# One decay matrix for both directions of the chunk outputs, D times x on VectorE, five buffers for chunk operands

## The chip, the cores and the metric

The kernel runs on one NeuronCore of a Trainium2 chip. The metric is device time in microseconds (us) of one execution. Engines are called as the profile calls them: PE (TensorE), DVE (VectorE), ACT (ScalarE), POOL (GpSimd), SP (the queue that issues nearly all DMAs).

## The reference, cut to what matters

The reference is one layer of a bidirectional diffusion trunk over 256 context and 1024 latent tokens: a combined input projection, three token mixers side by side (SSD, gated MLP, S5), an output projection and an MLP. The change lies in the SSD mixer alone, which runs a chunked scan once forward and once backward over chunks of 128 tokens. For one direction, chunk and head:

```python
seg = a_cum[:, :, :, None] - a_cum[:, :, None, :]
lmat = jnp.exp(jnp.where(lower, seg, -jnp.inf))
cb = jnp.einsum('bcqgn,bckgn->bcqkg', cm, bm)
y_diag = jnp.einsum('bcqkg,bcqkgr,bckgrp->bcqgrp', cb, lmat, x * dt)
chunk_states = jnp.einsum('bckgn,bckgr,bckgrp->bcgrpn', bm, decay_to_end, x * dt)
h_next = chunk_decay * h + chunk_states
y_off = jnp.einsum('bcqgn,bcgrpn,bcqgr->bcqgrp', cm, h_prev, jnp.exp(a_cum))
y = y_diag + y_off
```

The two directions have their own dt and decay, and the mixer's sum is y_forward + flip(y_backward) + D * x. There are 8 heads of 64 channels in two groups of 4 heads; B and C are shared by the heads of a group.

## The kernel before, in words

All matrices are kept with channels on the partitions. `xbc_slab` writes x, B and C of the whole sequence to the scratch tensor `xbc_d` in DRAM, `dt_chain` makes per-token decays: `DTD` (dt), `col` (cumulated decay as a column), `wdec` (decay to the end of the chunk; for the backward direction already times dt), `dtot` (decay of a whole chunk) and, in DRAM, `rows_d` (cumulated decay as rows).

`ssd_group(pool, g)` returns two generators for a group g. `right` walks over the chunks from the right and keeps the backward state at each boundary (`hb`). `outputs` walks over the 10 chunks from the left (`NCH`), makes y of a chunk in both directions and updates the forward state `hf`. For one chunk, `outputs` does this (lines 864 to 912):

- loads `xc` (x, B, C of the chunk: 4 x 128x128, 256 KB) and `rb` (rows of decay for two directions and 4 heads, spread over 128 partitions, 512 KB); `xc` and `rb` have three buffers each
- ACT makes `er`, the exponentials for the states' part (line 876); ACT and DVE form the smaller of the two directions' exponents, 4 instructions each (879, 880), ACT takes its exponential (881). The result in `rb[:, 1]` holds the forward decays above the diagonal and the backward ones below it
- PE transposes x and B (`tok_major`, `ps_wa`), and multiplies B by C (883)
- `cm` is that product under the two triangular masks (885); DVE and POOL each multiply the decays by one half of it (887), so that there is one matrix per direction and head; DVE makes `xd`, x times dt for both directions (889)
- PE sums in `py`: D times x through a diagonal matrix `diagd` (893), and for each direction and head one matmul with `xd` as weights (896); then the states' part in `po` (903)
- DVE scales `po` (905), adds `py` (906), POOL adds the second direction (908), and the result is stored to `y_d` (909)
- `new_state` updates the forward state, for which POOL weights `xd` by `wdec` (831)

The main program (lines 1043 to 1089) runs `outputs` of group 0 among the z products, the S5 products and the states of group 1, then `outputs` of group 1 among what is left of z and the first output products. `step(n)` puts n pieces of the adaLN product (a load of 256 KB of `ada_w` and four small matmuls, line 170) behind each chunk. A Python scheduler orders the instructions on each engine when the program is built (`schedule_with_timeline_sim`); on the chip each engine and the SP queue runs its own list in order, held by semaphores. An fp32 matmul leaves two records in the trace, a transpose one.

Of the kernel before, what the change touches and what calls it, by code (L numbers as in the profile page):

```python
# [10 lines left out]
F32 = mybir.dt.float32  # L11
# [31 lines left out]
def trunk_kernel(ctx: ExitStack, tc: tile.TileContext, I, O):  # L43
# [9 lines left out]
    def tt(out, a, b, op, eng=V):  # L53
        eng.tensor_tensor(out=out, in0=a, in1=b, op=op)  # L54
# [658 lines left out]
    def dt_chain():  # L713
# [36 lines left out]
        tt(wdec[:, 1], wdec[:, 1], DTD[:, 1], ALU.mult)  # L750
# [57 lines left out]
    def ssd_group(pool, g):  # L808
# [3 lines left out]
        def chunk_xbc(c, n):  # L812
            o = xoff(c)
            xc = pool.tile([128, 4, 128], F32, tag="xc", name="xc", bufs=3)[:, 0:n]
            load(xc, xbc_d[g, 0:n, :, o:o + 128].rearrange("a p n -> p a n"))
            return xc
# [12 lines left out]
        def new_state(tag, bufs, d, c, px, bt, h, name):  # L829
            xw = pool.tile([128, 4, 64], F32, tag="xw", name="xw", bufs=2)  # L830
            tt(xw, px, scal(wdec, d, c).unsqueeze(2).to_broadcast([128, 4, 64]), ALU.mult, V if d else G)
# [30 lines left out]
        def outputs():  # L862
            hf = None
            for c in range(NCH):
# [21 lines left out]
                for d, E in ((0, V), (1, G)):  # L886
                    tt(rb[:, d], rb[:, 1], cm[:, d].unsqueeze(1).to_broadcast([128, 4, 128]), ALU.mult, E)
                xd = pool.tile([128, 2, 4, 64], F32, tag="xd", name="xd", bufs=2)
                tt(xd, px.unsqueeze(1).to_broadcast([128, 2, 4, 64]),
                   DTD[:, :, c * 8 + g * 4:c * 8 + g * 4 + 4].unsqueeze(3).to_broadcast([128, 2, 4, 64]), ALU.mult)  # L890
                py = bank("wb", 2)[:, 0:256].rearrange("p (a q) -> p a q", a=2)
                for a in range(2):
                    T.matmul(py[:, a, :], lhsT=diagd[:, 2 * g + a, :], rhs=xc[:, a], start=True, stop=False)
                    for d in range(2):
                        for par in range(2):
                            T.matmul(py[par * 64:(par + 1) * 64, a, :], lhsT=xd[:, d, 2 * a + par],
                                     rhs=rb[:, d, 2 * a + par], start=False, stop=(d == 1))
# [8 lines left out]
                tt(cm, er[:, dirs[0]], py, ALU.add)  # L906
                if len(dirs) == 2:
                    tt(cm, cm, er[:, 1], ALU.add, G)
                load(y_d[g * 256:(g + 1) * 256].rearrange("(a p) n -> p a n", p=128)[:, :, c * 128:(c + 1) * 128], cm)
                if c < NCH - 1:  # L910
                    hf = new_state("hf", 2, 0, c, xd[:, 0], bt, hf, "hf")
# [131 lines left out]
    with tc.tile_pool(name="pd", bufs=1) as pd, banks("psB"):  # L1043
        diagd = pd.tile([128, 4, 128], F32, name="diagd")
        for i in range(4):
            G.tensor_scalar(out=diagd[:, i], in0=ident, scalar1=dcol[:, i:i + 1], scalar2=None, op0=ALU.mult)
# [546 lines left out]
```

## Time and profile before

| | us |
|---|---|
| median of 3 runs | 1590.81 (1589.42 to 1593.71) |
| the profiled execution | 1586.03 |
| its span in the trace | 1584.2 |
| PE busy in the span | 1459.8 (92%) |
| DVE busy | 1075.9 (68%) |
| ACT busy | 723.0 (46%) |
| POOL busy | 447.5 (28%) |
| mean busy share of the DMA engines' main queue | 46.9% |

The busy times are over the whole span, of which the changed part of the program takes some 210 us. A busy PE is not PE at its peak: its records overlap, and each stretch has a granted clock, 1.00 for 2.4 GHz and 0.50 for 1.2 GHz; a mean between them is a mixture. In a row of a group the count is followed by busy time, mean ns of one, and the idle time of the engine just before the group with what ended it. "L896" is line 896 of the kernel before; lines of small helpers (L54, L57, L60, L48) collect many operations, which the names tell apart.

### The profile page before, as it was taken

To read this page: it belongs to the slowest core of one execution; us is meant where nothing else is said; L and a number is where in the kernel's file an instruction comes from. 1 tells how busy PE (TensorE), PEld (TensorE's weight loads), DVE (VectorE), ACT (ScalarE), POOL (GpSimd) and SP (SyncE) were. 2 spreads that over 40 slices of the span, in tenths; PEclk is the share of its full clock that TensorE was granted. 3 is DMA by queue.
4 is the path that set the end of the run, shared out by engine and by line. 5 is a ranking of instruction groups with operands and counts; after the bars stand their busy time and mean duration, and the time that the engine had idled before them with its cause. 6 is when DMAs were issued, how large, how long until landed. Compare 5 with 4: busy or idle time off the path is not lost.

```text
span 1584.2 us, 24203 instructions
## 1 busy us (share of the span) xinstructions
PE 1459.8 (92%) x8664; PEld 1226.9 (77%) x8664; DVE 1075.9 (68%) x1807; ACT 723.0 (46%) x1428; POOL 447.5 (28%) x537
## 2 busy tenths in 40 slices
PE   4789988999897889989999999999899999999895
PEld 4677877877674668878888888888788988887795
DVE  5885587575755665558977765674554768979945
ACT  3565534463533533436655554455646333424322
POOL 4875376624333331321100000000240313032023
PEclk9699999999997889999999999999999999999897
DMA  9414546368778677446444443444844245415302
GB/s 325 141 68 135 179 149 192 86 182 216 208 261 210 204 246 235 121 123 192 130 156 150 149 141 116 137 140 141 264 132 161 67 160 171 123 54 180 113 34 100
DMA packets 238808, 249.12 MB, mean 157 GB/s; under 512 B 15808, under 2 KB 165344, under 8 KB 238688
## 3 DMA queue, kind: packets, MB, share of 16 engines
q1 hardware_dynamic: 222592, 230.32, 46.9%
q10 hardware_dynamic: 16096, 17.27, 3.2%
q8 instruction: 68, 1.11, 0.3%
q14 instruction: 52, 0.43, 0.1%
HBM read 178.63 MB, written 68.89 MB: 156 GB/s over the span
## 4 chain that ended last, share of the span: by engine, by line
PE 59%; DVE 8%; DMA 6%; issue 2%; ACT 2%; POOL 1%; SPq 0%; DVEq 0%; ACTq 0%; POOLq 0%
PE ps_w L1193 7%; PE ps_w L1194 7%; PE ps_w L1192 7%; PE ps_w L1349 6%; PE ps_w L1348 6%; PE ps_w L1350 6%; PE ps_mm L221 4%; PE ps_mm L219 4%; PE ps_mm L220 4%; DMA xc<-xbc_d 2%; DVE X L54 2%; PE ps_mm L1350 1%; PE ps_mm L1349 1%; PE ps_mm L1348 1%; DMA rb<-rows_d 1%
## 5 line engine op out<-in xcount | busy, mean ns | idle before, releaser
L219 PE MATMUL ps_mm<-hi,wh 128*128 128x512 f32 (+1 forms) x576 | 211.8, 368 | 6.4 <-DVE dtr L686 2.8
L221 PE MATMUL ps_mm<-hi,wl 128*128 128x512 f32 (+1 forms) x576 | 209.4, 364 | 0.9 <-DVE wl L54 0.9
L220 PE MATMUL ps_mm<-lo,wh 128*128 128x512 f32 (+1 forms) x576 | 209.8, 364 | 0.2 <-DVE lo L54 0.2
L1348 PE MATMUL ps_w<-uB,uA 128*128 128x512 f32 (+1 forms) x520 | 190.7, 371 | 9.3 <-ACT uB L60 8.9
L1349 PE MATMUL ps_w<-uB,uA 128*128 128x512 f32 (+1 forms) x520 | 191.7, 369 | 7.7 <-DVE uB L54 7.7
L1350 PE MATMUL ps_w<-uB,uA 128*128 128x512 f32 (+1 forms) x520 | 190.5, 367 | 0.0
L54 POOL TENSOR_TENSOR cb<-h 128x512 f32<-128x512 f32 x14 | 21.1, 1512 | 512.5 <-DMA h<-w 402.7
L219 PEld LDWEIGHTS ps_mm<-hi,wh 128*128 128x128 f32 x576 | 111.2, 193 | 24.7 <-DVE dtr L686 3.2
L221 PEld LDWEIGHTS ps_mm<-hi,wl 128*128 128x128 f32 x576 | 110.9, 193 | 19.1 <-issue 2.4
L220 PEld LDWEIGHTS ps_mm<-lo,wh 128*128 128x128 f32 x576 | 111.1, 193 | 15.9 <-issue 1.2
L1348 PEld LDWEIGHTS ps_w<-uB,uA 128*128 128x128 f32 x520 | 99.9, 193 | 25.4 <-ACT uB L60 9.3
L1349 PEld LDWEIGHTS ps_w<-uB,uA 128*128 128x128 f32 x520 | 100.1, 192 | 24.5 <-DVE uB L54 9.6
L1350 PEld LDWEIGHTS ps_w<-uB,uA 128*128 128x128 f32 x520 | 100.0, 192 | 15.4
L54 DVE TENSOR_TENSOR uB<-tb,uB 128x512 fp32r<-128x512 f32 x106 | 88.7, 857 | 13.5 <-ACT uB L60 13.5
L60 ACT ACTIVATE uB<-tb 128x512 fp32r<-128x512 f32 x106 | 65.6, 625 | 62.1 <-PE ps_w L1350 31.7
L54 DVE TENSOR_TENSOR wl<-wraw,wh 128x1024 fp32r<-128x1024 f32 x32 | 50.3, 1572 | 40.6 <-ACT wh L60 40.2
L54 DVE TENSOR_TENSOR X<-X,ps_w 128x512 f32<-128x512 f32 x84 | 56.1, 680 | 27.7 <-PE ps_w L1350 27.6
L54 DVE TENSOR_TENSOR q<-q,ps_w 128x512 f32<-128x512 f32 x48 | 32.9, 686 | 60.2 <-PE ps_w L1194 59.5
L60 ACT ACTIVATE c<-c 128x512 f32<-128x512 f32 x64 | 40.3, 629 | 56.9 <-DVE c L54 55.9
L54 POOL TENSOR_TENSOR sq<-sq 128x512 f32<-128x512 f32 (+1 forms) x31 | 41.1, 1331 | 81.8 <-ACT sq L60 81.3
L1350 PE MATMUL ps_mm<-ch,uA 128*128 128x256 f32 x224 | 63.2, 283 | 0.0
L1349 PE MATMUL ps_mm<-cl,uA 128*128 128x256 f32 x224 | 63.2, 283 | 0.0
(430 smaller groups left out, 3993.9 us busy)
## 6 DMA issues: line engine op xcount, KB each, us to landing
rw<-w SPq DMA_DIRECT2D x112, 256.0 KB
tb<-a_d SPq DMA_DIRECT2D x106, 256.0 KB
aw<-ada_w SPq DMA_DIRECT2D x64, 256.0 KB
h<-w SPq DMA_DIRECT2D x32, 512.0 KB
a_d<-t SPq DMA_DIRECT2D x42, 256.0 KB
rb<-rows_d SPq DMA_DIRECT2D x20, 512.0 KB
adaw<-ada_w SPq DMA_DIRECT2D x32, 256.0 KB
wraw<-w_out SPq DMA_DIRECT2D x16, 512.0 KB
```

Of the source, the lines that this page charges most:

```text
L54: eng.tensor_tensor(out=out, in0=a, in1=b, op=op)
L60: S.activation(out=out, in_=in_, func=func, **kw)
L219: T.matmul(out, lhsT=wh(k), rhs=xh(k), start=(k == 0), stop=False)
L220: T.matmul(out, lhsT=wh(k), rhs=xl(k), start=False, stop=False)
L221: T.matmul(out, lhsT=wl(k), rhs=xh(k), start=False, stop=(k == nk - 1))
L1192: T.matmul(out, lhsT=wh, rhs=X[0][:, j, :], start=(j == 0), stop=False)
L1193: T.matmul(out, lhsT=wh, rhs=X[1][:, j, :], start=False, stop=False)
L1194: T.matmul(out, lhsT=wl, rhs=X[0][:, j, :], start=False, stop=(j == 3))
L1348: T.matmul(out, lhsT=wh, rhs=bh, start=start, stop=False)
L1349: T.matmul(out, lhsT=wh, rhs=bl, start=False, stop=False)
L1350: T.matmul(out, lhsT=wl, rhs=bh, start=False, stop=stop)
```

## The change

It makes one matrix per head out of both directions' halves, with dt in it: ACT scales the forward half of `cm` by the forward dt of each token, DVE adds the backward half times its dt, 4 instructions of 128x128 each, and one DVE product with the decays follows. x goes to PE as it is, through a copy by ACT (`xs`). D times x leaves PE: DVE adds it to `py` with two instructions per chunk. POOL now adds the two directions of the states' part before DVE adds them to the rest. The weighting `xw` of the forward state moves from POOL to DVE and reads x from PSUM, and `wdec` carries dt for both directions. `diagd` goes. `xc` has five buffers.

```diff
--- before.py
+++ after.py
@@ -747,7 +747,7 @@
         S.copy(col[:, 0], pc[:, 0:80])
         act(col[:, 1], pc[:, 80:160], ACT.Copy, scale=-1.0)
         act(wdec.rearrange("p d c -> p (d c)"), pc[:, 160:320], ACT.Exp)
-        tt(wdec[:, 1], wdec[:, 1], DTD[:, 1], ALU.mult)
+        tt(wdec, wdec, DTD, ALU.mult)
         act(dtot.rearrange("p d c -> p (d c)"), pc[:, 320:480], ACT.Exp)
         pr = bank("ad")
         for d in range(2):
@@ -811,7 +811,7 @@
 
         def chunk_xbc(c, n):
             o = xoff(c)
-            xc = pool.tile([128, 4, 128], F32, tag="xc", name="xc", bufs=3)[:, 0:n]
+            xc = pool.tile([128, 4, 128], F32, tag="xc", name="xc", bufs=5)[:, 0:n]
             load(xc, xbc_d[g, 0:n, :, o:o + 128].rearrange("a p n -> p a n"))
             return xc
 
@@ -828,7 +828,7 @@
 
         def new_state(tag, bufs, d, c, px, bt, h, name):
             xw = pool.tile([128, 4, 64], F32, tag="xw", name="xw", bufs=2)
-            tt(xw, px, scal(wdec, d, c).unsqueeze(2).to_broadcast([128, 4, 64]), ALU.mult, V if d else G)
+            tt(xw, px, scal(wdec, d, c).unsqueeze(2).to_broadcast([128, 4, 64]), ALU.mult)
             pst = bank("ws")[:, 0:256]
             T.matmul(pst, lhsT=bt, rhs=xw.rearrange("p h e -> p (h e)"), start=True, stop=True)
             hn = pool.tile([128, 256], F32, tag=tag, name=name, bufs=bufs)
@@ -883,18 +883,19 @@
                 T.matmul(pcb, lhsT=xc[:, 2], rhs=xc[:, 3], start=True, stop=True)
                 cm = pool.tile([128, 2, 128], F32, tag="cm", name="cm", bufs=2)
                 tt(cm, pcb.unsqueeze(1).to_broadcast([128, 2, 128]), tri[:, 0:2], ALU.mult)
-                for d, E in ((0, V), (1, G)):
-                    tt(rb[:, d], rb[:, 1], cm[:, d].unsqueeze(1).to_broadcast([128, 4, 128]), ALU.mult, E)
-                xd = pool.tile([128, 2, 4, 64], F32, tag="xd", name="xd", bufs=2)
-                tt(xd, px.unsqueeze(1).to_broadcast([128, 2, 4, 64]),
-                   DTD[:, :, c * 8 + g * 4:c * 8 + g * 4 + 4].unsqueeze(3).to_broadcast([128, 2, 4, 64]), ALU.mult)
+
+                d0, d1 = scal(DTD, 0, c), scal(DTD, 1, c)
+                for hh in range(4):
+                    act(rb[:, 0, hh], cm[:, 0], ACT.Copy, scale=d0[:, hh:hh + 1])
+                    stt(rb[:, 0, hh], cm[:, 1], d1[:, hh:hh + 1], rb[:, 0, hh], ALU.mult, ALU.add)
+                tt(rb[:, 1], rb[:, 1], rb[:, 0], ALU.mult)
+                xs = pool.tile([128, 4, 64], F32, tag="xs", name="xs", bufs=2)
+                S.copy(xs, px)
                 py = bank("wb", 2)[:, 0:256].rearrange("p (a q) -> p a q", a=2)
                 for a in range(2):
-                    T.matmul(py[:, a, :], lhsT=diagd[:, 2 * g + a, :], rhs=xc[:, a], start=True, stop=False)
-                    for d in range(2):
-                        for par in range(2):
-                            T.matmul(py[par * 64:(par + 1) * 64, a, :], lhsT=xd[:, d, 2 * a + par],
-                                     rhs=rb[:, d, 2 * a + par], start=False, stop=(d == 1))
+                    for par in range(2):
+                        T.matmul(py[par * 64:(par + 1) * 64, a, :], lhsT=xs[:, 2 * a + par], rhs=rb[:, 1, 2 * a + par],
+                                 start=True, stop=True)
                 hs_ = (hf, hb[c])
                 dirs = [d for d in range(2) if hs_[d] is not None]
                 po = bank("wb", 2).rearrange("p (d a q) -> p d a q", d=2, a=2)
@@ -903,12 +904,14 @@
                         T.matmul(po[:, d, a], lhsT=hs_[d][:, a * 128:(a + 1) * 128], rhs=xc[:, 3], start=True, stop=True)
                 ds = slice(dirs[0], dirs[-1] + 1)
                 tt(er[:, ds], po[:, ds], er[:, ds], ALU.mult)
-                tt(cm, er[:, dirs[0]], py, ALU.add)
+                for a in range(2):
+                    stt(cm[:, a], xc[:, a], dcol[:, 2 * g + a:2 * g + a + 1], py[:, a], ALU.mult, ALU.add)
                 if len(dirs) == 2:
-                    tt(cm, cm, er[:, 1], ALU.add, G)
+                    tt(er[:, 0], er[:, 0], er[:, 1], ALU.add, G)
+                tt(cm, cm, er[:, dirs[0]], ALU.add)
                 load(y_d[g * 256:(g + 1) * 256].rearrange("(a p) n -> p a n", p=128)[:, :, c * 128:(c + 1) * 128], cm)
                 if c < NCH - 1:
-                    hf = new_state("hf", 2, 0, c, xd[:, 0], bt, hf, "hf")
+                    hf = new_state("hf", 2, 0, c, px, bt, hf, "hf")
                 yield
 
         return right(), outputs()
@@ -1041,9 +1044,6 @@
         u_slab(m)
     psA.close()
     with tc.tile_pool(name="pd", bufs=1) as pd, banks("psB"):
-        diagd = pd.tile([128, 4, 128], F32, name="diagd")
-        for i in range(4):
-            G.tensor_scalar(out=diagd[:, i], in0=ident, scalar1=dcol[:, i:i + 1], scalar2=None, op0=ALU.mult)
         (right0, out0), (right1, out1) = [ssd_group(pd, g) for g in range(2)]
         ada = (x for q in range(4, 12) for x in adaln(q, lambda: pd.tile([128, 512], F32, tag="aw", name="aw", bufs=2), 512))
```

The scheduler makes a new order of it. SP at the third chunk of group 1 (its rb is `rb_5098` before, `rb_5129` after; the fourth chunk's `rb_5259`, after `rb_5293`). Before:

```order
L48 DMA xc_5096<-xbc_d_76 128x4x128
L48 DMA rb_5098<-rows_d_84 128x2x512
L48 DMA aw_5004<-ada_w 128x512
L48 DMA aw_5010<-ada_w 128x512
L48 DMA y_d_75<-cm_4493 128x2x128
L48 DMA xc_5257<-xbc_d_76 128x4x128
L48 DMA rb_5259<-rows_d_84 128x2x512
```

After:

```order
L48 DMA rb_5046<-rows_d_84 128x2x512
L48 DMA xc_5127<-xbc_d_76 128x4x128
L48 DMA aw_5038<-ada_w 128x512
L48 DMA xc_5291<-xbc_d_76 128x4x128
L48 DMA aw_5100<-ada_w 128x512
L48 DMA y_d_75<-cm_4407 128x2x128
L48 DMA aw_5106<-ada_w 128x512
L48 DMA aw_5112<-ada_w 128x512
L48 DMA aw_5118<-ada_w 128x512
L48 DMA rb_5129<-rows_d_84 128x2x512
L48 DMA xc_5374<-xbc_d_76 128x4x128
```

Before, xc and rb of a chunk are issued side by side. Now xc of the third and fourth chunk (`xc_5127`, `xc_5291`) stand ahead of the third chunk's rb, and that of the fifth (`xc_5374`) right behind it.

PE at the outputs of the third chunk of group 1 (its py is `ps_wb_5125` before, `ps_wb_5163` after). Before:

```order
L896 MATMUL ps_wb_5125<-rb_5098,xd_5123 64x128 x2
L833 MATMUL ps_ws_5147<-xw_5145,bt_5116 128x256
L170 MATMUL ps_ad_5003<-aw_5081,sc_108 32x128 x4
L896 MATMUL ps_wb_5125<-rb_5098,xd_5123 64x128 x2
L893 MATMUL ps_wb_5125<-xc_5096,diagd_3133 128x128
L896 MATMUL ps_wb_5125<-rb_5098,xd_5123 64x128 x4
L903 MATMUL ps_wb_5136<-xc_5096,h0_5094 128x128 x2
L903 MATMUL ps_wb_5136<-xc_5096,hb_4549 128x128 x2
```

After:

```order
L833 MATMUL ps_ws_5181<-xw_5179,bt_5147 128x256
L824 MATMUL ps_wa_5390<-pk1_88,xc_5374 128x128 x3
L897 MATMUL ps_wb_5163<-rb_5129,xs_5161 64x128 x4
L904 MATMUL ps_wb_5168<-xc_5127,h0_5125 128x128 x2
L904 MATMUL ps_wb_5168<-xc_5127,hb_4574 128x128 x2
L883 MATMUL ps_wa_5390<-xc_5374 128x128
L170 MATMUL ps_ad_5203<-aw_5356,sc_108 32x128 x4
```

The diagonal products (L893) are gone from between the others, and one block of four matmuls is left of L896 (now L897); the states' part follows as before (L903, now L904).

DVE at the third chunk of group 1 (`rb_5098` and `cm_5119`, after: `rb_5129` and `cm_5150`). Before:

```order
L54 TENSOR_TENSOR cm_5119<-ps_wa_5112,pk2_90 128x256
L54 TENSOR_TENSOR xd_5123<-ps_wa_5112,DTD_129 128x512
L54 TENSOR_TENSOR hf_5066<-hf_5066,ps_ws_5064 128x256
L54 TENSOR_TENSOR rb_5098<-rb_5098,cm_5119 128x512
L57 SCALAR_TENSOR_TENSOR rb_5259<-rb_5259,col_130 128x128 x4
L54 TENSOR_TENSOR cm_5039<-er_5020,ps_wb_5045 128x256
L54 TENSOR_TENSOR hf_5149<-hf_5149,ps_ws_5147 128x256
L54 TENSOR_TENSOR er_5100<-ps_wb_5136,er_5100 128x512
L54 TENSOR_TENSOR cm_5280<-ps_wa_5273,pk2_90 128x256
L54 TENSOR_TENSOR xd_5284<-ps_wa_5273,DTD_129 128x512
L54 TENSOR_TENSOR cm_5119<-er_5100,ps_wb_5125 128x256
```

After:

```order
L54 TENSOR_TENSOR cm_5150<-ps_wa_5143,pk2_90 128x256
L54 TENSOR_TENSOR hf_5097<-hf_5097,ps_ws_5095 128x256
L57 SCALAR_TENSOR_TENSOR rb_5293<-rb_5293,col_130 128x128 x2
L57 SCALAR_TENSOR_TENSOR rb_5129<-cm_5150,DTD_129,rb_5129 128x128 x3
L57 SCALAR_TENSOR_TENSOR cm_5067<-xc_5044,pk2_90,ps_wb_5080 128x128 x2
L57 SCALAR_TENSOR_TENSOR rb_5129<-cm_5150,DTD_129,rb_5129 128x128
L54 TENSOR_TENSOR xw_5179<-ps_wa_5143,wdec_131 128x256
L57 SCALAR_TENSOR_TENSOR rb_5293<-rb_5293,col_130 128x128
L54 TENSOR_TENSOR er_5048<-ps_wb_5085,er_5048 128x256
L57 SCALAR_TENSOR_TENSOR rb_5293<-rb_5293,col_130 128x128
L54 TENSOR_TENSOR rb_5129<-rb_5129 128x512
L54 TENSOR_TENSOR cm_5067<-cm_5067,er_5048 128x256
```

`xd` is gone, and between `cm` and the product with the decays stand the four new instructions and `xw`; the instructions of neighbouring chunks lie between them as before.

## Rows read from the trace of the kernel before

**Rows 1.** Windows: busy us (instructions) per engine, granted clock, DMA share, GB/s

```profile
core 0: us, PE busy (x) PEld busy (x) DVE busy (x) ACT busy (x) POOL busy (x), PEclk, DMA share, GB/s
370.00:480.00 110.00, 101.00 (x752) 74.29 (x751) 64.76 (x132) 46.02 (x105) 39.14 (x43) 0.99 0.76 227
480.00:580.00 100.00, 86.22 (x668) 59.56 (x670) 63.58 (x132) 45.49 (x103) 38.59 (x42) 0.81 0.76 219
```

**Rows 2.** Timeline of SP: start, us; first, tenth and twentieth store of y_d

```profile
383.75 0.38 SPq L48 DMA_DIRECT2D y_d<-cm  x1
486.80 0.38 SPq L48 DMA_DIRECT2D y_d<-cm  x1
578.65 0.37 SPq L48 DMA_DIRECT2D y_d<-cm  x1
```

**Rows 3.** Waits of PE, 370 to 580 us: us in total, times, longest

```profile
PE ps_wa L824 <- DMA xc<-xbc_d: 7.9, 6, 2.7
```

**Rows 4.** Chain that ended last, 370 to 580 us: shares; start, us, piece

```profile
by line: DMA xc<-xbc_d 13.8%; DMA rb<-rows_d 9.7%; PE ps_wb L896 8.9%; PE ps_mm L640 4.3%; PE ps_wb L903 4.3%; PE ps_wb L893 4.2%; PE ps_ws L833 4.2%; DMA aw<-ada_w 4.0%; PE ps_ad L170 3.6%; PE ps_wa L824 3.3%; PE ps_mm L221 3.3%; PE ps_mm
488.70 6.99 DMA rb<-rows_d
```

**Rows 5.** Groups, 370 to 480 us: count | busy us, mean ns | idle before

```profile
L896 PE MATMUL ps_wb<-rb,xd 128*64 128x128 f32 x144 | 13.4, 290 | 0.2 <-POOL rb L54 0.2
L893 PE MATMUL ps_wb<-xc,diagd 128*128 128x128 f32 x36 | 8.1, 308 | 0.0
L54 DVE TENSOR_TENSOR xw<-ps_wa,wdec 128x256 f32<-128x256 f32 x9 | 3.7, 415 | 1.6 <-ACT bt L826 1.6
```

**Rows 6.** Groups, 480 to 580 us

```profile
L896 PE MATMUL ps_wb<-rb,xd 128*64 128x128 f32 x176 | 20.2, 339 | 2.1 <-DVE rb L54 2.1
L893 PE MATMUL ps_wb<-xc,diagd 128*128 128x128 f32 x40 | 11.4, 372 | 0.6 <-DVE er L54 0.6
L57 DVE SCALAR_TENSOR_TENSOR rb<-rb,col 128x128 f32<-128x128 f32 x36 | 17.1, 511 | 2.9 <-ACT rb L60 2.7
L54 DVE TENSOR_TENSOR rb<-rb,cm 128x512 f32<-128x512 f32 x10 | 9.5, 954 | 0.0
L54 DVE TENSOR_TENSOR xd<-ps_wa,DTD 128x512 f32<-128x512 f32 x10 | 6.8, 678 | 0.0
L54 DVE TENSOR_TENSOR cm<-er,ps_wb 128x256 f32<-128x256 f32 x11 | 4.5, 411 | 1.4 <-PE ps_wb L896 1.4
L54 POOL TENSOR_TENSOR rb<-rb,cm 128x512 f32<-128x512 f32 x10 | 12.9, 1288 | 5.7 <-DVE rb L54 2.8 <-ACT rb L60 0.9 <-issue 0.7
L54 POOL TENSOR_TENSOR xw<-xd,wdec 128x256 f32<-128x256 f32 x9 | 6.0, 663 | 21.8 <-DVE xd L54 21.8
L60 ACT ACTIVATE rb<-rb,col 128x128 f32<-128x128 f32 x36 | 12.0, 391 | 0.1
L836 ACT COPY hf<-ps_ws 128x256 f32<-128x256 f32 x1 | 0.4, 352 | 0.0
```

**Rows 7.** Tile rb, whole span: duration ns min/median/max, first and last start

```profile
L57 DVE SCALAR_TENSOR_TENSOR rb<-rb,col x80: 326/346/1468, 327.3 to 563.0; 128x128 f32<-128x128 f32 x80
L54 DVE TENSOR_TENSOR rb<-rb,cm x20: 676/876/1758, 374.9 to 570.9; 128x512 f32<-128x512 f32 x20
```

**Rows 8.** Timeline of PE: start, us, records

```profile
487.17 0.44 PE L896 MATMUL ps_wb<-rb,xd 128*64 128x128 f32 x4
487.54 0.49 PE L893 MATMUL ps_wb<-xc,diagd 128*128 128x128 f32 x2
503.99 0.70 PE L896 MATMUL ps_wb<-rb,xd 128*64 128x128 f32 x4
504.62 0.80 PE L893 MATMUL ps_wb<-xc,diagd 128*128 128x128 f32 x2
```

**Rows 9.** Windows of 5 us, columns as in rows 1

```profile
485.00:490.00 5.00, 3.88 (x39) 2.65 (x38) 1.55 (x5) 1.09 (x4) 3.03 (x4) 1.00 0.84 214
500.00:505.00 5.00, 5.00 (x37) 2.60 (x36) 1.32 (x4) 0.63 (x1) 0.61 (x1) 0.50 0.64 136
```

## Prediction, written before the changed kernel ran

> **What bounds the kernel now.** Everything that the edit touches runs between 370 and 580 us of the span, so I read the windows first. Up to 480 us, while the chunks of group 0 run among the z, S5 and context products, PE is busy 101.0 of 110 us at a granted clock of 0.99; from 480 to 580 us, where group 1 runs with little else on PE, it is busy 86.2 of 100 us at 0.81, and the DMA engines have a share of 0.76 in both [rows 1]. The stores of y_d count the chunks: the first is issued at 383.75 us, the tenth at 486.80, the twentieth at 578.65, so a chunk takes 103.05 / 9 = 11.5 us in the first stretch and 91.85 / 10 = 9.2 in the second [rows 2]. Of the waits that PE itself has there, the longest in sum is for the load of xc, 7.9 us in 6 waits [rows 3]. The chain that ended last is made of much the same: transfers of xc are 13.8% of its 210 us and those of rb 9.7%, and of the matmuls in it L896 and L893 are 8.9 and 4.2% [rows 4]. So PE is the first bound, and loads of a chunk's operands the second. Outside these 210 us the order moves little, and I cost it at nothing.
>
> **PE, the part that falls away.** Per chunk, 2 matmuls with diagd (two records each) and 8 of 16 with the decay matrices go; the order shows them gone, so that the edit does what it says isn't in doubt. In the first stretch L893 is busy 8.1 us and L896 13.4 [rows 5]; in the second 11.4 and 20.2 [rows 6]. Gone are 8.1 + 13.4 / 2 = 14.8 and 11.4 + 20.2 / 2 = 21.5 us, together **36.3 us** of PE.
>
> **Five buffers for xc.** In the order the load of a chunk's xc now stands two chunks ahead of the load of its rb, where it stood right beside it. Its buffer is also held longer, since VectorE reads it for D times x after the matmuls. I let the 7.9 us of PE's waits [rows 3] be what is to be had; with rb still in three buffers the floor is 0. PE and xc together: **at most 44.2 us**.
>
> **VectorE, second stretch.** It is busy 63.6 us [rows 1]. Four scalar_tensor_tensor of 128x128 per chunk are added, 40 in all. The same instruction on rb has a median of 346 ns [rows 7], but a mean of 511 in this stretch [rows 6], where POOL is busy 38.6 us [rows 1]. At 346 they cost 13.8. The xw of the forward state comes over from POOL: 9 x 415 ns [rows 5] = 3.7. D times x is 20 instructions on 128x128 with a PSUM operand; no row has one, and its ends are 346 [rows 7] and the 411 of cm<-er,ps_wb, twice as long [rows 6]; nearest in size is the first, so 20 x 350 = 7.0. The last sum, 128x256, lies between 346 [rows 7] and 676 [rows 7], I take the 411 of the same size: 4.1. Off go xd 6.8 and the old cm<-er 4.5 [rows 6]. POOL loses 12.9 + 6.0 us of its 38.6 [rows 6], and if the stts on rb then fall to 346 and the big product from 954 to its least, 676 [rows 6, 7], 36 x 0.165 + 10 x 0.278 = 8.7 more come off. Net +8.6: **72.2 us**. At today's dearer prices throughout (511 for all sixty new stts, 676 for the sum, nothing given back) it is 63.6 - 11.3 + 20.4 + 3.7 + 10.2 + 6.8 = **93.4 us**. I take the first, because what is removed on POOL is what stood beside these instructions.
>
> The Trainium skill's page "SBUF — State Buffer", section "Who interferes with whom", says that a VectorE instruction with two SBUF inputs and a GpSimd instruction that reads SBUF shut each other out for their whole length. This trace agrees: an stt of 326 ns at least takes up to 1468 [rows 7]. By that rule half of POOL's work that stays would still block half as much, VectorE would need about 83 us, and my sum would be some 5 us smaller.
>
> **ScalarE, POOL, DMA, second stretch.** ScalarE gains 40 scaled copies at 391 ns and 10 copies of x from PSUM at 352 [rows 6], 15.6 + 3.5 on 45.5 [rows 1]: 64.6. POOL falls to 19.7; its sum er0 + er1 is the size of the old cm + er. diagd itself (4 operations ahead of the stage, on POOL, which there waits for other work) and the doubled product on wdec, once, count nothing: should their cover go, each is under 3 us once. Bytes are unchanged, 0.76 x 100 = 76 us of all DMA engines. One new order of waits: ScalarE's scaled copies need cm, which needs the chunk's xc and two matmuls; behind them on ScalarE stand the exponentials of the next chunk. Before, only the copy bt tied ScalarE to a chunk's xc. The x in PSUM is also held until ScalarE has copied it, so a late cm now holds a bank as well.
>
> **The sum.** Second stretch: PE 86.2 - 21.5 = 64.7, VectorE 72, ScalarE 65, DMA 76. The stretch is now 100 / 86.2 = 1.16 times its busiest engine. At 1.16 the new one is 88 us; four engines this close wait on each other more, and at 1.25 it is 95. I take 91: **-9**. First stretch: PE 101.0 - 14.8 = 86.2, DMA 0.76 x 110 = 83.6, VectorE 64.8 + 8.6 = 73.4. The factor is 1.09 now; at 1.09 it gives 94, at 1.16 100. I take 99, near the second, since DMA comes up to PE: **-11**. Together -20 us, ends -15 and -28. The profiled execution took 1586.0 us, the median of the runs is 1590.8, 4.8 more; so 1566 for an execution like the profiled one and **1571 us** against the median. A measurement of this kernel tells about 0.3% (4.8 us) from no change.
>
> **The rivals.**
> - *All of it comes home.* PE is what bounds both stretches and the others adapt: -44, 1547 us. For: PE's 92% in the first stretch. Against: the DMA engines, at 0.76 now [rows 1], would go to 0.76 x 210 / 166 = 0.96. Chance 0.12.
> - *PE cools.* In the second stretch PE goes on at 1.2 GHz throughout, because it waits more. At granted 1.00 and 0.50 [rows 9] four records of L896 take 0.44 and 0.70 us, two of L893 0.49 and 0.80 [rows 8], a factor of 1.6. A mean of 0.81 means 38% of the time at the lower level already; of the 64.7 us the other 62% would grow by 0.6: 64.7 + 24 = 89, times 1.16 = 103, +3; with -11 of the first stretch 1583 us. For: in 485 to 490 us PE was idle 1.1 of 5 us, and by 500 the lower level stood [rows 9]. Against: xc, which ends several of those waits, comes earlier. The skill's page "TensorE: Matmul & The Clock Gate", section "HAM oscillation", says just this of kernels whose bursts are shorter than their waits for loads: less work then runs slower. Chance 0.10.
> - *The loads keep the pace.* The same bytes per chunk pass the same engines, rb has three buffers, and a load of rb took 6.99 us from issue on [rows 4]. If what xc gains rb loses, the chunks stay at 9.2 and nearly 11.5 us; the gain is 0 to 5, 1588 us. Chance 0.13.
> - *VectorE takes PE's place: slower.* Its queue is in order, its new instructions are short, and POOL's remaining products still stand against them. At the dear prices the second stretch is 93.4 x 1.16 = 108 us, +8; the first has 64.8 + 29.8 = 94.6, times 1.16 = 110, no gain: 1599 us. It decides from 100 / 1.16 = 86 us of VectorE in the second stretch, that is two thirds of the way between the two prices, a mean of about 0.455 us for an stt. For: 0.511 is what it pays now. Against: half of POOL goes. Chance 0.13.
>
> **How the numbers follow.** My forecast has 0.52, with 1563 to 1576 as its own range. Faster by over 0.3% (under 1586): 0.52 + 0.12 + 0.10 = 0.74; within: 0.13; slower: 0.13. The range 1550 to 1596 takes in the forecast, the cool PE and the loads, and cuts most of the first and of the last rival, some 0.2.
>
> **What would show it.** PE's busy time down by some 36 us with L893 and half of L896 gone; PE's waits for xc nearly gone; y_d stores closer, about 10.3 and 8.4 us apart; VectorE about 72 us in a stretch of some 91; stts on rb near 0.35 us. I am wrong if the chunks of group 1 keep 9.2 us though PE is idle (then it is loads, or ScalarE standing behind cm), if stts stay above 0.45 us (VectorE), or if PE's granted clock in that stretch falls to near 0.5 (clock).

## The result, and the profile after

The changed kernel took **1597.55 us** (median of 6 runs, 1594.81 to 1603.53) beside 1589.11 for the kernel before: a ratio of 1.0053, 95% interval 1.0032 to 1.0074. It is slower by half a per cent; forecast was 1571, and the range ended at 1596. The profiled execution has a span of 1593.0 us, 8.8 more than before.

The windows of the changed kernel, columns as in [rows 1]:

```profile
370.00:480.00 110.00, 90.30 (x627) 65.61 (x626) 66.20 (x177) 59.21 (x148) 18.86 (x22) 0.91 0.79 224
480.00:580.00 100.00, 69.84 (x524) 48.60 (x523) 68.73 (x189) 59.59 (x154) 18.13 (x22) 0.76 0.73 212
```

PE lost 10.7 and 16.4 us of busy time in these windows, ScalarE gained 13 to 14, POOL lost 20, and no engine is busy for more than 82% of a window. The granted clock fell from 0.99 to 0.91 and from 0.81 to 0.76. The same three stores as in [rows 2], timeline of SP:

```profile
387.21 1.40 SPq L48 DMA_DIRECT2D y_d<-cm  x1
499.60 0.38 SPq L48 DMA_DIRECT2D y_d<-cm  x1
596.54 0.37 SPq L48 DMA_DIRECT2D y_d<-cm  x1
```

A chunk now takes (499.60 - 387.21) / 9 = 12.5 us in group 0 and 96.94 / 10 = 9.7 in group 1, where it took 11.5 and 9.2. The last store is 17.9 us late; half of that is gone again by the end of the span. Waits from 370 to 580 us (releaser: us in total, times, longest), first three of the kernel before:

```profile
ACT er L60 <- DMA rb<-rows_d: 37.2, 12, 6.4
DVE rb L57 <- ACT rb L60: 16.0, 8, 4.3
PE ps_ad L170 <- DMA aw<-ada_w: 3.0, 3, 1.6
```

The same three of the changed kernel, and its chain as in [rows 4]:

```profile
ACT er L60 <- DMA rb<-rows_d: 31.5, 11, 5.1
PE ps_ad L170 <- DMA aw<-ada_w: 29.4, 15, 5.0
DVE rb L57 <- ACT rb L60: 29.1, 13, 6.0
```

```profile
by line: DMA rb<-rows_d 24.5%; DVE rb L57 11.4%; DMA aw<-ada_w 7.8%; DMA y_d<-cm 5.7%; issue 5.2%; ACT er L60 5.1%; ACT rb L60 4.1%; DMA mx<-mix_d 2.9%; PE ps_wb L897 2.6%; PE ps_wb L904 2.5%; DVE cm L54 2.4%; PE ps_ws L833 2.3%; PE ps_ad L
```

PE's waits for xc are gone, as meant, and transfers of xc (13.8% of the chain before) are no longer among its longest. In their place PE waits for aw, 29.4 us where it was 3.0. Transfers of rb have gone from 9.7 to 24.5% of the chain, and the VectorE instructions `scalar_tensor_tensor` (stts) on rb, which the row of [rows 4] doesn't name, to 11.4%. ScalarE's wait for rb is not new: it was 37.2 us before and is 31.5 now. VectorE's wait behind it, for ScalarE's rb, grew from 16.0 to 29.1. The instructions themselves cost what I had put down; groups of 480 to 580 us, as in [rows 6]:

```profile
L57 DVE SCALAR_TENSOR_TENSOR rb<-cm,DTD,rb 128x128 f32<-128x128 f32 x40 | 13.3, 375 | 0.0
L60 ACT ACTIVATE rb<-cm,DTD 128x128 f32<-128x128 f32 x40 | 12.8, 391 | 3.8 <-DVE cm L54 3.7
L57 DVE SCALAR_TENSOR_TENSOR rb<-rb,col 128x128 f32<-128x128 f32 x36 | 12.0, 368 | 6.5 <-ACT rb L60 6.5
L57 DVE SCALAR_TENSOR_TENSOR cm<-xc,pk,ps_wb 128x128 f32<-128x128 f32 x22 | 6.5, 337 | 1.2 <-PE ps_wb L897 1.1
```

### The profile page after: what moved, and what is told of

Its sections match the earlier page's. It is cut to its first block, busy times and chain, and to the rows that moved or that the text cites. A ratio compares the mean times of both kernels' runs of the same rounds, so it can differ in the third digit from the quotient of the medians.

```text
span 1593.0 us, 23865 instructions
## 1 busy us (share of the span) xinstructions
PE 1436.1 (90%) x8424; PEld 1210.8 (76%) x8424; DVE 1085.1 (68%) x1925; ACT 751.4 (47%) x1528; POOL 402.6 (25%) x495
## 4 chain that ended last, share of the span: by engine, by line
PE 54%; DVE 10%; DMA 8%; ACT 3%; issue 2%; POOL 0%; SPq 0%; DVEq 0%; ACTq 0%; POOLq 0%
PE ps_w L1194 7%; PE ps_w L1193 7%; PE ps_w L1192 7%; PE ps_w L1348 6%; PE ps_w L1349 6%; PE ps_w L1350 6%; PE ps_mm L221 3%; PE ps_mm L219 3%; DMA rb<-rows_d 3%; PE ps_mm L220 3%; DVE rb L57 2%; PE ps_mm L1350 1%; PE ps_mm L1349 1%; PE ps_mm L1348 1%; DVE X L54 1%
## 5 line engine op out<-in xcount | busy, mean ns | idle before, releaser
L219 PE MATMUL ps_mm<-hi,wh 128*128 128x512 f32 (+1 forms) x576 | 212.1, 368 | 10.3 <-ACT xr L791 3.9
L220 PE MATMUL ps_mm<-lo,wh 128*128 128x512 f32 (+1 forms) x576 | 209.3, 363 | 1.1 <-DVE lo L54 1.1
L1349 PEld LDWEIGHTS ps_w<-uB,uA 128*128 128x128 f32 x520 | 100.3, 193 | 24.5 <-DVE uB L54 9.6
L54 DVE TENSOR_TENSOR wl<-wraw,wh 128x1024 fp32r<-128x1024 f32 x32 | 47.5, 1484 | 37.4 <-ACT wh L60 37.2
L1350 PE MATMUL ps_mm<-ch,uA 128*128 128x256 f32 x224 | 63.2, 283 | 0.0
L1348 PE MATMUL ps_mm<-ch,uA 128*128 128x256 f32 x224 | 63.1, 283 | 0.0
```

Of the source, the lines that this page charges most:

```text
L219: T.matmul(out, lhsT=wh(k), rhs=xh(k), start=(k == 0), stop=False)
L220: T.matmul(out, lhsT=wh(k), rhs=xl(k), start=False, stop=False)
L1348: T.matmul(out, lhsT=wh, rhs=bh, start=start, stop=False)
L1349: T.matmul(out, lhsT=wh, rhs=bl, start=False, stop=False)
L1350: T.matmul(out, lhsT=wl, rhs=bh, start=False, stop=stop)
```

## The experiments

All ratios are to the kernel before, timed beside the run on the same chip; e1 to e18 are the runs in the order in which they were made. Where an expectation counts 8 matmuls per chunk, these are records, two to a matmul.

### The yardstick, and what order alone does

> The changed kernel itself, as a yardstick on the same chip as the three runs beside it: the ratio to the kernel before was 1.0053 (1.0032 to 1.0074) from 6 runs. If the loss is real it comes again at 1.003 to 1.008; if it was what a few runs scatter, it is within 1.000 to 1.003, and then all that was read against 1.0053 counts for less.

Measured: 1.0025 (1.0005 to 1.0046), 1592.21 us. The loss is there again, smaller. I take the changed kernel to be at 1.0025 to 1.0053, 4 to 8 us slower, and compare with both ends.

```diff
+                xs = pool.tile([128, 4, 64], F32, tag="xs", name="xs", bufs=2)
+                S.copy(xs, px)
                 d0, d1 = scal(DTD, 0, c), scal(DTD, 1, c)
...
-                xs = pool.tile([128, 4, 64], F32, tag="xs", name="xs", bufs=2)
-                S.copy(xs, px)
```

> The changed kernel with the copy of x written ahead of the building of the weights instead of behind it. The work is the same, to the instruction; only the order on the engines' queues comes out otherwise (about a quarter of VectorE's rows move). If the order alone moves the time by as much as the change did, the ratio differs from the 1.0025 to 1.0053 of the changed kernel by 0.003 or more, either way. If order hardly counts and work and buffers do, it stays within 1.002 to 1.006.

Measured: 1.0055 (1.0030 to 1.0081). Against 1.0025 that is 0.003, against 1.0053 nothing: not told apart. But it sets a caution for all that follows: each edit, however small, is re-ordered on all engines, and a difference of some 0.3% between two versions is not to be put down to what was edited. How much more an order can be worth was not measured.

### PE's work: taken away alone, and put back

In the kernel before, only this:

```diff
-                    T.matmul(py[:, a, :], lhsT=diagd[:, 2 * g + a, :], rhs=xc[:, a], start=True, stop=False)
-                    for d in range(2):
-                        for par in range(2):
-                            T.matmul(py[par * 64:(par + 1) * 64, a, :], lhsT=xd[:, d, 2 * a + par],
-                                     rhs=rb[:, d, 2 * a + par], start=False, stop=(d == 1))
+                    for par in range(2):
+                        T.matmul(py[par * 64:(par + 1) * 64, a, :], lhsT=xd[:, 0, 2 * a + par],
+                                 rhs=rb[:, 0, 2 * a + par], start=True, stop=True)
```

> The kernel before with the matmuls that the change takes away left out, the 2 of D and the 8 of the second decay matrix per chunk, and nothing put in their place: 36.3 us of PE by my own sum. It leaves out D times x and the part of the reversed direction inside a chunk; the product on POOL for that direction is still made. This is the first term of the forecast by itself. If PE bounds the two stretches as I held, the time falls by 20 to 36 us, ratio 0.977 to 0.987, and what the change adds on VectorE and ScalarE ate the gain. If PE's 0.92 and 0.86 busy share was work that stretches to fill a time set by the loads and the in-order queues, it falls by 0 to 8 us, ratio 0.995 to 1.000, and the term itself was worth little.

Measured: **0.9931** (0.9905 to 0.9957), 0.0069 x 1589 = 11 us faster. Between the two expectations: PE's 36.3 us were worth 11 (7 to 15 by the interval), three tenths, in the one order that this edit got. Its windows:

```profile
370.00:480.00 110.00, 94.00 (x673) 69.37 (x671) 62.32 (x138) 49.56 (x112) 41.56 (x44) 0.95 0.82 238
480.00:580.00 100.00, 73.87 (x576) 54.39 (x569) 68.93 (x138) 46.68 (x103) 39.98 (x41) 0.81 0.75 221
```

From 480 us on PE is busy 73.87 of 100 us, beside a share of 0.75 of the DMA engines. The other way round, in the changed kernel:

```diff
-                        T.matmul(py[par * 64:(par + 1) * 64, a, :], lhsT=xs[:, 2 * a + par], rhs=rb[:, 1, 2 * a + par],
-                                 start=True, stop=True)
+                        for _ in range(2):
+                            T.matmul(py[par * 64:(par + 1) * 64, a, :], lhsT=xs[:, 2 * a + par],
+                                     rhs=rb[:, 1, 2 * a + par], start=True, stop=True)
```

> The changed kernel with each matmul of the decay matrix made twice, both times from the start, so that PE gets back about half of the work that was taken away (8 matmuls per chunk, 16.6 us by the row of L897) and nothing else changes. If PE's work sets these stretches (my forecast's premise), the time rises by 10 to 18 us, to 1607 to 1616 us, a ratio of about 1.011 to 1.017 to the kernel before. If PE is off the path and the waits of loads and of VectorE and ScalarE set it, it rises by 0 to 5 us, ratio 1.005 to 1.009. If the clock is what was lost (PE idles, the granted clock falls to 0.76 in 480 to 580 us), more work on PE holds the clock up and the time falls, ratio under 1.003 with a granted clock over 0.85 there.

Measured: 0.9998 (0.9982 to 1.0014), 4 to 9 us *faster* than the changed kernel with 16.6 us more for PE; the granted clock in 480 to 580 us is 0.81. So these 16.6 us cost no time. PE's busy time in the span didn't even grow (1436.5 us, where it was 1436.1), which goes with the higher clock of the second stretch. The profiled execution, the slowest of the 12 at 1598.35 us, has its last store at 606.76, 10.2 us later than the changed kernel, so its chunks came no closer. With `range(5)`:

> The changed kernel with each matmul of the decay matrix made five times: 64 more per chunk pair of records, some 66 us more of PE (4 x 16.6 by the row of L897), more than the change took away. If PE had 25 us and more of free time in each stretch (it is busy 90.3 of 110 and 69.8 of 100 us, the rest is waits for loads), the first 30 to 40 us cost little and the time rises by 15 to 35 us: ratio 1.015 to 1.027. If PE sets the time after all: by over 55 us, ratio 1.04. If the granted clock is what PE's idle time costs, 480 to 580 us shows a clock over 0.95 and the rise stays under 15 us: ratio under 1.012.

Measured: 1.0184 (1.0154 to 1.0214), so 66 us of PE cost 21 to 25 us. Its windows:

```profile
370.00:480.00 110.00, 103.64 (x848) 81.83 (x847) 64.86 (x172) 56.26 (x143) 16.79 (x21) 1.00 0.74 214
480.00:580.00 100.00, 77.98 (x692) 63.62 (x691) 61.17 (x163) 51.75 (x135) 15.89 (x18) 0.86 0.65 181
```

Busier, PE gets the higher clock (1.00 and 0.86) and pays part of the extra work with it: its busy time in the span grew by 39.9 us (1436.1 to 1476.0), not by 66. Less work went with a lower clock in the changed kernel, and in e13 up to 480 us alone (0.95, then 0.81 as before). How much time that gave back was not separated.

### What the change adds: taken away alone

```diff
-                d0, d1 = scal(DTD, 0, c), scal(DTD, 1, c)
-                for hh in range(4):
-                    act(rb[:, 0, hh], cm[:, 0], ACT.Copy, scale=d0[:, hh:hh + 1])
-                    stt(rb[:, 0, hh], cm[:, 1], d1[:, hh:hh + 1], rb[:, 0, hh], ALU.mult, ALU.add)
-                tt(rb[:, 1], rb[:, 1], rb[:, 0], ALU.mult)
+                tt(rb[:, 1], rb[:, 1], cm[:, 0].unsqueeze(1).to_broadcast([128, 4, 128]), ALU.mult)
```

> The changed kernel without the building of the weights: the 4 scaled copies on ScalarE and the 4 stts on VectorE per chunk are left out, and the decay matrix is multiplied by the mask product of one direction (dt and the other direction are left out). 25.5 us less on ScalarE, 26.6 us less on VectorE, and the chain inside rb is shorter by some 3 us per chunk. If these additions are what ate the gain of PE, the time falls to the forecast, about 1567 to 1575 us, ratio 0.985 to 0.991. If the stage is set by loads and by the order of the queues, ratio 0.996 to 1.002.

Measured: 0.9980 (0.9955 to 1.0006), 7 to 12 us better than the changed kernel, with runs from 1576.56 to 1595.22 us. The building of the weights costs about what PE's lost work gives, but without it the kernel is still far from 1571. Its first, tenth and twentieth store:

```profile
387.67 2.05 SPq L48 DMA_DIRECT2D y_d<-cm  x1
488.65 0.39 SPq L48 DMA_DIRECT2D y_d<-cm  x1
568.97 0.38 SPq L48 DMA_DIRECT2D y_d<-cm  x1
```

11.2 and 8.0 us per chunk, in group 1 closer than the 8.4 that I forecast for the change, in group 0 not (10.3). Its last store is 27.6 us earlier than that of the changed kernel; in the profiled executions 15.4 us of that are left at the end (1579.38 beside 1594.81), and by the ratios 7 to 12. Then the scaled copies on VectorE instead of ScalarE:

```diff
-                    act(rb[:, 0, hh], cm[:, 0], ACT.Copy, scale=d0[:, hh:hh + 1])
+                    V.tensor_scalar(out=rb[:, 0, hh], in0=cm[:, 0], scalar1=d0[:, hh:hh + 1], scalar2=None, op0=ALU.mult)
```

> The changed kernel with its four scaled copies per chunk made by VectorE instead of ScalarE: no hand-over between the engines inside the weight matrix, 25.5 us less on ScalarE, about 80 x 0.2 to 0.35 = 16 to 28 us more on VectorE. If the hand-overs are what holds rb (R in its narrow form: VectorE waits 36.2 us for ScalarE's rb, was 16.0), the time falls by 5 to 12 us, to 1585 to 1592 us. If VectorE is close to the bound itself, it rises by 5 to 15 us, to 1603 to 1612 us. By X and A nothing over 4 us.

Measured: 1.0034 (1.0017 to 1.0051), where the changed kernel is. The edit removes the hand-overs, takes load off ScalarE (46.97 instead of 59.59 us in 480 to 580) and puts some on VectorE (72.20 instead of 68.73) all at once, so that a gain and a loss may cancel. But it shortens two of the waits that stand out above: ScalarE's wait for rb falls from 31.5 to 18.4 us, VectorE's behind it from 29.1 to 16.6, rb is gone from the head of the chain, and the time does not move.

### Buffers and loads

How long a buffer of rb is held can be read from two timelines: the issue of its load on SP, and the end of the last matmul on PE that reads it. In the kernel before:

```profile
515.51 1.12 PE L896 MATMUL ps_wb<-rb,xd 128*64 128x128 f32 x8
516.71 0.36 SPq L48 DMA_DIRECT2D rb<-rows_d  x1
```

The matmuls end at 516.63, and the load that takes over the buffer is issued 0.08 us later. Of the 17 loads that take over a buffer, 13 are issued within 0.5 us of its release before, and 8 after. From issue to release a buffer is held 33.7 us (mean of chunks 4 to 10 of group 0) and 29.6 (group 1) before, 35.4 and 29.4 after. So the three buffers set the start of rb's loads in the kernel before already, and the change made the hold 1.7 us longer in group 0 and no longer in group 1. What it added is lateness at the start of the stage: the load issued at 396.94 comes 8.7 us after its buffer is free (388.24), right behind the store `ssdo<-hf` (396.51) on SP. Before, that store was issued at 384.23, and the load of the same chunk, the fifth, at 387.05, 0.5 us after the release. That is the new order, and not the work; what it costs was not measured by itself.

e1 to e3, e6, e7 and e15 change buffer counts of the changed kernel. First xc:

```diff
-            xc = pool.tile([128, 4, 128], F32, tag="xc", name="xc", bufs=5)[:, 0:n]
+            xc = pool.tile([128, 4, 128], F32, tag="xc", name="xc", bufs=3)[:, 0:n]
```

> The changed kernel with the buffers of xc back at three. Three theories of why the change lost 8 us although PE has 23.7 us less to do: R, the rb loop: the new chain ScalarE copy, VectorE stt, four times over, keeps each of the three rb buffers longer, so the loads of rb are issued later, and the chunks come no closer than the loads. X, the xc loads: with five buffers they are issued early and stand in front of the loads of rb and aw, so what xc gains rb and aw lose. A, the aw loads: SP issues in order, a load of aw stands behind the other loads, and PE waits for it (31.8 us in 17 waits between 310 and 640 us). By X this edit gives the loss back: about 1589 us, and PE's waits for aw and the chain's rb pieces shrink. By R nothing is gained and PE's waits for xc (7.9 us before) come back: 1598 to 1606 us. By A no more than 3 us either way: 1595 to 1600 us.

Measured: 1.0018 (0.9997 to 1.0038). PE's waits for xc are back (8.6 us) and the time is no worse, rather a little better: the five buffers bought nothing. VectorE's wait for ScalarE's rb is 13.5 us here, less than half of the changed kernel's 29.1, at about the same time. With four of rb as well:

```diff
-                rb = pool.tile([128, 2, 4, 128], F32, tag="rb", name="rb", bufs=3)
+                rb = pool.tile([128, 2, 4, 128], F32, tag="rb", name="rb", bufs=4)
```

> The changed kernel with three buffers of xc and, with the room that frees, four of rb. By R this is the cure: a load of rb is issued a chunk earlier, about 10 us, which is more than the 7 us it takes; the waits of ScalarE for rb (38.6 us, 13 times) fall below 15 us, and the time falls to 1570 to 1580 us. By X it is about 1586 to 1590 us, like three buffers of xc alone. By A, PE goes on waiting for aw some 30 us and the time stays within 4 us of the run with three buffers of xc alone.

> The version with three buffers of xc and four of rb again, with other neighbours: 0.9963 (0.9941 to 0.9986) the first time. If the fourth rb buffer is worth what it showed, the ratio is again 0.994 to 0.998. If such differences are mostly the chance of one session, it comes out within 0.999 to 1.003.

Measured: **0.9963** (0.9941 to 0.9986) and, the second time, 0.9966 (0.9945 to 0.9987): 9 us better than with three, and better than the kernel before. The waits and the chain of the first of the two, 370 to 580 us:

```profile
PE ps_ad L170 <- DMA aw<-ada_w: 20.6, 10, 6.4
PE ps_wa L824 <- DMA xc<-xbc_d: 14.8, 6, 3.5
DVE rb L57 <- ACT rb L60: 7.9, 13, 2.6
```

```profile
by line: DMA aw<-ada_w 12.1%; DMA xc<-xbc_d 8.3%; PE ps_wb L904 6.9%; PE ps_mm L219 6.4%; PE ps_mm L220 6.4%; PE ps_mm L221 6.3%; DMA h<-ssd 5.8%; PE ps_ad L170 5.3%; PE ps_ws L833 4.7%; PE ps_wa L824 4.1%; PE ps_wb L897 3.5%; DMA y_d<-cm 3
```

ScalarE's wait for the load of rb (27.7 us with three) is not there any more, VectorE's wait behind it fell from 13.5 to 7.9, and rb is gone from the head of the chain (13.0% with three); aw and xc lead it now. Beside e1 the chunks come closer, from 11.9 to 11.4 and from 10.9 to 10.1 us, and the last store is 11.3 us earlier (589.36). Yet it is 10.7 us later than in the kernel before, whose span is 2.7 us longer: the pace of the chunks alone does not give the time. The second run repeats the same order, and does not tell the buffer from the order. Four buffers of aw (`bufs=2` to 4, xc at three):

> The changed kernel with three buffers of xc and, with the room that frees, four of aw. By A the loads of aw are issued ahead of need, PE's waits for aw fall from 31.8 to under 10 us, the granted clock in 370 to 580 us goes back over 0.9 and the time falls to 1575 to 1585 us. By R and X the work on ada_w is only filling, and the time is within 4 us of the run with three buffers of xc alone.

Measured: 0.9997 (0.9978 to 1.0015). Between 310 and 640 us PE's waits for aw fell to 5.6 us as expected, but its waits for xw of VectorE rose from 6.7 to 16.2; the gain over three xc buffers alone is 3 to 4 us, and the intervals overlap. Four of rb with three of aw, and four of rb with four of er, both with the states of the two groups in one set of 16 buffers (`f"hb{g}", 9` becomes `"hb", 16`):

> The changed kernel with three buffers of xc, four of rb and three of aw, the room taken from the right-to-left states of the two groups, which now share 16 buffers instead of 9 and 9. Two loops were cured one at a time: rb gave 10 us, aw 4. If they are independent bounds that take each other's place, both together give more than either: ratio 0.988 to 0.993. If the rb loop was the only one that counts, it stays at the 0.996 of four rb buffers alone.

> The changed kernel with three buffers of xc, four of rb and four of er, room from the same sharing. With four rb buffers ScalarE no longer waits for loads of rb, but 12.2 us in 9 waits for the sum that frees er. If er has become the bound, its fourth buffer gives 3 to 8 us: ratio 0.991 to 0.994. If aw and xc (22.6 and 14.8 us of PE's waits) are the next bounds, it stays near 0.996.

Measured: 0.9988 (0.9972 to 1.0004) and 1.0051 (1.0029 to 1.0074). The first is not told apart from four rb buffers alone (the intervals overlap), the second is worse. In the first ScalarE's wait for rb is gone, in the second it is 34.5 us in spite of the fourth buffer. In both profiles the first chunk's store comes at 396 to 397 us instead of 386, and the order is another; what the buffers alone do is not told by these two. Half the bytes of aw:

```diff
+            h = W // 2 if W == 512 else W
-            load(w, I["ada_w"][k * 128:(k + 1) * 128, q * W:(q + 1) * W])
+            load(w[:, 0:h], I["ada_w"][k * 128:(k + 1) * 128, q * W:q * W + h])
...
-                         rhs=w[:, i * n:(i + 1) * n], start=(k == 0), stop=(k == 7))
+                         rhs=w[:, i * n % h:i * n % h + n], start=(k == 0), stop=(k == 7))
```

> The changed kernel with half the bytes in each load of aw (128 KB instead of 256; the matmuls read the half that is there twice, so the modulation is computed from half of its weights, and PE's work and the number of loads stay). Of the 64 such loads 16 MB, some 8 MB fall away, at 212 to 224 GB/s about 37 us of all the DMA engines' time in 310 to 600 us, which are busy 0.73 to 0.79 there. If the loads' bytes bound the stage (the DMA engines have no more to give), the time falls by 10 to 20 us, ratio 0.993 to 0.999, PE's waits for aw under 12 us. If the latency of each load and the few buffers bound it, by 3 to 8 us: 1.000 to 1.003. If it is VectorE's and ScalarE's queues, by under 3 us.

Measured: 1.0045 (1.0024 to 1.0066), no gain. The profiled execution is 8.9 us late already at its first store (396.10), and from there to the last it takes 213.8 us, where the changed kernel took 209.3. So the bytes of these loads aren't what holds the kernel at its time.

### The parts by themselves

D times x on VectorE in the kernel before (`diagd` and its matmuls go, the two stts and the changed sums of the diff come), with four buffers of rb, for which the states share 16 buffers as in e6, and with three, where they do not:

> The kernel before with two decay matrices as it was, D times x on VectorE, so that the matrix of D falls away, and four buffers of rb (room from that matrix and from the shared states). If the new chain of scaled copies and stts is what holds rb too long, the kernel before doesn't need the fourth buffer, and only D's 9 to 10 us of PE count: ratio 0.994 to 1.000. If the loads of rb bound the kernel before just as well, it gains as much here as the changed one did, 8 to 12 us, and D's part on top: ratio 0.985 to 0.993; one matrix would then be worth nothing or less.

> The kernel before with only one part of the change: D times x on VectorE, so 2 matmuls less per chunk (19.5 us of PE by the rows of L893) and 20 short stts and a third sum more on VectorE; two decay matrices, three buffers of rb and of xc as before. With a fourth rb buffer this was 1.0001 (0.9982 to 1.0021). If the fourth buffer gives this kernel nothing, because its rb is freed soon enough, the ratio is again 0.998 to 1.002. If the fourth buffer was worth 10 us here too, it is 1.004 to 1.008. By the price that PE's work had when it was taken away alone (11 us for 36) the 19.5 us are worth 6, ratio 0.996, unless VectorE takes them back.

Measured: 1.0001 (0.9982 to 1.0021) with four, 0.9983 (0.9962 to 1.0004) with three. So with two matrices this version with a fourth buffer is no faster, though ScalarE's wait for rb is gone there too (29.7 us with three, none with four). What the shared states cost was not measured alone, and e6, e7 and e18, which share them as well, all came out above e2; so it isn't shown that the buffer itself gives nothing here. The chain with four:

```profile
by line: DMA aw<-ada_w 20.5%; PE ps_wb L902 7.0%; DMA y_d<-cm 6.7%; PE ps_wb L895 6.5%; PE ps_mm L219 5.4%; PE ps_ad L170 5.2%; DMA z<-z_d 5.2%; PE ps_mm L220 5.1%; PE ps_mm L221 5.0%; issue 4.8%; PE ps_ws L833 4.1%; SPq L48 4.0%; DMA yf<-y
```

aw and PE stand behind rb. Two variants of the best version: xw back on POOL, made from `xs`; and D times x back on TensorE (xc at three, rb at four, states shared):

> The best version so far, three buffers of xc and four of rb (0.9963), with xw of the forward state back on POOL, made from the copy of x in SBUF: VectorE gets rid of 18 x 415 ns = 7.5 us and of one place in its queue, and the x in PSUM is held by the copy alone. PE's waits for xw were 5.2 us there (3.1 with POOL before the change). If VectorE's queue is the next bound, ratio 0.990 to 0.994; if loads are, 0.995 to 0.998; if POOL's xw, slower and standing against VectorE, costs more than it gives, over 0.998.

> The changed kernel with D times x back on TensorE (the matrix of D, started in the same bank), three buffers of xc and four of rb, states shared in 16 buffers. VectorE loses 20 stts and a sum, 15 us, PE gains 19.5, xc is free after PE. If what counts is VectorE's queue and the hold of the buffers, and PE's work is worth only a third of its length, this beats the 0.9966 of four rb buffers alone: 0.990 to 0.995. If PE's work counts as much as VectorE's, it comes out at 0.996 to 1.000.

Measured: 1.0048 (1.0025 to 1.0072) and 1.0004 (0.9982 to 1.0026), beside 0.9963 to 0.9966: the first is worse, the second looks it, with intervals that just touch. PE's waits for xc are 18.8 us in the first, while ScalarE's wait for rb is gone as in e2, and it is no faster than the changed kernel: an end to that wait alone does not bring the gain. So neither move helps the best version; whether it is the place of the work or the new order that costs, the runs don't separate.

## Why the prediction was wrong

- **The step that failed is the sum**, its rule that a stretch is 1.16 to 1.25 times its busiest engine, with PE as that engine before. It let 36.3 us of PE, with ScalarE and VectorE loaded in return, come out as -20. In the changed kernel the windows are 110 / 90.3 = 1.22 and 100 / 73 = 1.37 times their busiest (PE, and the DMA engines), where 1.09 to 1.16 and 1.16 to 1.25 were put down. PE taken away alone gives -11 (e13), the building of the weights takes back 7 to 12 (e14), and five buffers of xc give nothing (e1 against the changed kernel). If these parts add up, which was not tested, that sums to about zero; the measured +4 to +8 is 0.25 to 0.5% off it.
- *"So PE is the first bound"*: a busy share of 0.92 and 0.86 didn't show it. PE took 16.6 us more, by the row of L897, without loss (e5). The Trainium skill's page "Perfetto Trace Analysis", section "Identifying the Most-Contended Engine", warns that for TensorE the busy share of matmuls is no good measure of how close a kernel is to its limit. e13 and e5 show that it is no measure of what the work is worth either: three tenths of a microsecond per microsecond, and none. The prediction looked at PE's waits alone; ScalarE's 37.2 us for rb stood in the same trace, and there too the loads of rb were issued as their buffers came free.
- *PE -36.3*: the instructions went, but PE's busy time fell by only 23.7 in the whole span (1459.8 to 1436.1), which fits the lower clock for what is left.
- *Five buffers for xc, up to 7.9 us*: the waits went, the time did not. PE waited for aw instead, and transfers of rb, 13.0% of the chain with three buffers of xc, were 24.5% with five.
- *The prices of the new instructions* were right, near the cheap end: stts on rb at 368 and 375 ns, D times x at 337, copies at 391. VectorE had 68.7 of 100 us where I had 72 of 91. The fall from 511 ns with POOL's 38.6 us to 368 with 18.1 is what I forecast.
- *The new order of waits* was named (scaled copies need cm, the next chunk's exponentials stand behind them) and priced at nothing. VectorE's wait for ScalarE grew by 13 us, but that is no price either: it is 13.5 us in e1 and 16.6 in e4, and both take about the time of the changed kernel. The hold of rb's buffers hardly grew. The fourth buffer gave 9 us in one version (e2, e15 against e1); as other versions with it did not keep them (e7 and e12, less clearly e6 and e18), it is not shown that rb's buffers are what the loss comes from.
- *The rivals*: "the loads keep the pace" named rb's three buffers, and rb's loads do follow their release, before as after; but it had no more than a zero for the loss. "VectorE takes PE's place" had nearly the right time, 1599, by luck: its stts stayed far under the 455 ns from which it was to decide, and more VectorE work, with less for ScalarE, cost nothing (e4). "PE cools" is there in part (0.81 to 0.76, 0.99 to 0.91). One of my own signs of error came true: chunks of group 1 at 9.2 us or more while PE is idle. It named loads or ScalarE behind cm as the cause; the runs don't decide between them.
- *Open*: what makes the kernel 4 to 8 us slower rather than equal; how much of it is the clock, and how much the new order with its late loads of rb; why chunks that come closer (e14) are not worth all of it at the end.

## What to carry to other kernels

Before pricing work that an engine loses, see what a run with that work left out gives: in a stage where three engines and the DMAs were some 45 to 90% busy it was worth three tenths of its length. Read the waits of all engines, not only those of the busiest one, and see which loads are issued as soon as a buffer is free, as those of rb were here before the change. Two more buffers of xc, whose wait headed PE's list, gave nothing; the same 4 KB per partition for rb gave 9 us, in one version. A wait that shrinks is not yet time that is won. Differences of 0.3% between versions that a scheduler orders anew need a repeat, and a version with the same work in another order, before they get a cause.

## What was unexpected of the hardware

More work made PE faster where it had idled: with 66 us of added matmuls the granted clock rose from 0.91 and 0.76 to 1.00 and 0.86, and only 21 to 25 us appeared in the time. The Trainium skill's page "TensorE: Matmul & The Clock Gate", section "HAM oscillation", describes the same from the other side, matmul bursts shorter than the waits for their loads bringing the low clock back. The traces agree in that the clock of 480 to 580 us fell from 0.81 to 0.76 while PE's waits for aw there rose from 3.0 to 17.9 us; whether its bursts are shorter than these waits was not measured. And loads of aw with half the bytes (128 KB) left the time where it was.
